# Queries and keys of a head pair kept in three orders, copied on GpSimd, so that attention scores are read with unit step

## The chip, the core and the metric

The kernel runs on one core of a Trainium2 chip. A core has five engines that work side by side, each through its own queue in order: TensorE (PE, matrix products; its weight loads are shown apart as PEld), VectorE (DVE), ScalarE (ACT), GpSimd (POOL), and SyncE (SP), which here mostly issues transfers (DMA) between HBM and the on-chip memory SBUF. Products land in PSUM, a small accumulator memory. The metric is the device time of one execution in microseconds (us).

## The reference

One encoder layer over a prompt of 256 and a sample of 2048 tokens with the same weights. After an input projection, half of the columns go through a Hyena mixer (two long convolutions, done here by Fourier transforms as matrix products), the other half through dilated attention. The attention is what the change touches:

```python
DILATED_BRANCHES = ((128, 1), (512, 4), (2048, 16))
def by_residue(a):
    return a.reshape(B, Ls, dilation, H, E).transpose(0, 2, 1, 3, 4)
...
s = jnp.einsum('brnqhe,brnkhe->brnhqk', qb, kb).astype(jnp.float32) * (E ** -0.5)
...
s = jnp.where(valid[None, None, :, None], s + bias[None, None, None], NEG_INF)
m = jnp.max(s, axis=-1, keepdims=True)
p = jnp.exp(s - m)
```

There are 8 heads of 64 channels. In a branch with dilation d, token t attends to tokens with the same residue t mod d, within a window. So the branches read queries and keys with step 1, 4 and 16. The three outputs are merged by their softmax denominators, joined with the Hyena half, normed, projected and fed to a gated feed-forward.

## The kernel before

Code is written as generators that `weave` emits side by side; a scheduler then fixes the order of each engine's queue. After the input projection the attention (`attention`) and the Hyena convolutions (`hyena`) are woven; the output projection (`output`) and the feed-forward follow. The output works in nine blocks of 256 tokens: the first is the prompt, and the other eight need the finished Hyena result of the sample.

**Attention.** Heads are taken in four pairs (`hp`), each pair in three branches (`b`). A pair and a branch make a section of 18 blocks of 128 queries. Of these, 16 belong to the sample and two to the prompt; in the first branch all read with step 1, in the second the sample's read with step 4 and in the third with step 16. The prompt's two blocks in the second branch are "packed" ones read with step 2, and so are those of the third.

`prepare` loads queries and keys of a head, channel by token, into three tiles of 128 partitions and 2304 columns: `Qh` (rounded queries), `Ql` (the rest) and `Ks` (keys, rounded on half of the partitions, the rest on the other half). It works in four chunks of 576 columns: transfers on SP, a rounding on ACT (L861, L864), differences on DVE (L201, tile Ql) and POOL (L201, tile Ks), a cast on DVE (L866). The next pair is prepared during the current one, a step every sixth block. The tiles of one pair lie in one place, those of the next in another, so that two sets exist.

`scores` makes a block: per head two matmuls into tile aS (L901 with Qh as weights and Ks moving, L902 with Ql), then a sum with the bias and its minimum on DVE (L905, to tile aP), and the exponential with its sum on ACT (L908). aS has two buffers. `flip` transposes aP on PE (L917, tile aT) and copies it out on ACT or DVE; `values` multiplies by the values (L932, tile aOp); `tokens` transposes back (L945, aOT) and stores.

**Hyena.** For each convolution, `hyena_first` is the first transform step: DVE casts and a POOL difference (L201, tile hS), matmuls L689 and L690, a copy, a store. `hyena_second` goes through groups: 32 for the sample, 4 for the prompt. A group has the product hs2k (L720, the filter's spectrum), a scaling on DVE (L722, tile hK), the product hs2z (L724, the signal's), four DVE products (L728 to L731, into tiles t1 and t2, both shown as ht), their addition on POOL (L732), and the first inverse step hs3 on PE (L738) with a copy on ACT. hs2k and hs2z share two PSUM buffers, and t2 has one. Then a last step per row of the inverse: L775 on PE (hs4), L776 on DVE. The second convolution starts when the first one's result has gone through all its first steps. Two groups share one load each of the transform's table (htab), the signal (hx) and the filter (hk) and one store of hbe; hx, hk, hbe and the last step's hD are tiles of 128 partitions by 2 by 512 in float32. A last step also loads the gate and stores the result, each half as large as hD.

Of the kernel before, what the change touches and what calls it, by code (L numbers as in the profile page):

```python
# [21 lines left out]
P = 128  # L22
# [10 lines left out]
# ---------------------------------------------------------------- constants of the shapes  # L33
# [106 lines left out]
# ---------------------------------------------------------------- host layout  # L140
# [46 lines left out]
# ---------------------------------------------------------------- the kernel  # L187
class Hybrid:
# [20 lines left out]
    # ---- constants that live through the whole kernel  # L209
# [33 lines left out]
    # ---- emission of several parts of the kernel side by side  # L243
    def weave(self, streams, until=None):
        """streams: [[generator, yields expected, yields so far]]; ends with `until`, or with all of them."""
# [12 lines left out]
    # ---- modulation: columns of silu(c) @ ada_w + ada_b for one of the six parts  # L258
# [10 lines left out]
    def ada_tensor(self, pool, psp):  # L269
        """Part 1 and the first half of part 0 on the tensor engine."""  # L270
# [25 lines left out]
    def ada_vector(self, s, pool, rows, bufs, ms=range(8)):  # L296
        """Part s on the vector engine, from the transposed weights."""
# [10 lines left out]
    # ---- Hyena filters: position MLP, decay, norm, spectrum  # L308
# [157 lines left out]
    # ---- input projection  # L466
    # a sub-block: (first column of xT, number of columns)
# [30 lines left out]
    def input_rstd(self, wp, w2, psp, p):  # L498
        """1 / rms over the channels of x, on every partition, for the columns that pass p is the first to use."""
# [19 lines left out]
    def first_input(self, wp, w2, psp):  # L519
        """Normed x of the first pass, with its 1 / rms."""  # L520
# [18 lines left out]
    def modulate(self, X, both=False):  # L539
        """x * (gain * (1 + scale)) + shift."""  # L540
# [21 lines left out]
    def split(self, hp, X, H):  # L562
        """hi + lo = x."""
# [20 lines left out]
    def project(self, hp, wp, w2, psp, ms, H=None):  # L584
        """Columns `ms` (in chunks of 128) of the input projection, for all tokens; H: input of the first pass."""
# [77 lines left out]
    # ---- Hyena: long convolutions of one request and one order  # L663
    def time_major(self, t, r, q):
        """Rows token = n2c * i + nh * h + q, q + 1 of a token-major DRAM tensor, by h as [i, 2, c]."""
        off, L = REQ[r]
        nh = L // 128
        v = t[off:off + L].rearrange("(i h n) c -> h i n c", h=2, n=nh)
        return [v[h, :, q:q + 2] for h in range(2)]
# [6 lines left out]
    def hyena_first(self, wp, psp, r, An, n, z):  # L676
        """First DFT step, over the rows of z, for the columns n and n + 1 of each half."""
# [17 lines left out]
    def hyena_second(self, wp, psp, r, o, A, B):  # L695
        """Second DFT step of the signal and of the filter, their product, first inverse step."""
# [988 lines left out]
```

## Time and profile before

| what | value |
|---|---|
| time, three runs | 3507.36, 3507.86 (median), 3508.28 us |
| span of the profiled execution | 3512.3 us |
| PE busy | 3281.4 us, 93% |
| DVE busy | 2633.7 us, 75% |
| ACT busy | 1548.2 us, 44% |
| POOL busy | 1430.0 us, 41% |
| attention with Hyena beside it | 945 to 1646 us of the span |

The profile lists no time of the profiled execution other than its span, which is 0.13% over the median. A busy PE is not PE at its peak: matmuls are pipelined, so the duration of one overlaps the next, and a matmul's price is read from its start to the start of what follows. Shares over the whole span mix stages with different limits; the stretch from 945 to 1646 us is the one to look at.

### The profile page before, as it was taken

What the parts mean: (1) busy time and instruction counts of PE and PEld (TensorE: products, weight loads), DVE (VectorE), ACT (ScalarE), POOL (GpSimd) and SP (SyncE); (2) the same over time, 40 slices, a digit from 0 to 9 for tenths busy, and PEclk for the clock granted to TensorE, in tenths of its full rate; (3) what the DMA queues carried; (4) which work ended last, traced back from release to release, by engine and by line L of the source; (5) the groups of instructions that cost most, each with busy time, mean ns of one, the idle gap of its engine ahead of it and who ended that gap; (6) DMA issues with size and microseconds to landing.
All of it is one profiled execution on the core that took longest, in us unless ns stands there. A gap on an engine that the chain in (4) does not pass through costs nothing.

```text
span 3512.3 us, 57891 instructions
## 1 busy us (share of the span) xinstructions
PE 3281.4 (93%) x21142; PEld 2941.1 (84%) x21142; DVE 2633.7 (75%) x4490; ACT 1548.2 (44%) x3190; POOL 1430.0 (41%) x1110
## 2 busy tenths in 40 slices
PE   7999899899899899998899899999899999899998
PEld 4987788789756666565799799999899999899998
DVE  7988878765487667685887878888887878567657
ACT  4576743323254665455554433223332324344433
POOL 1487761124231332220444555545655555223222
PEclk9999999999999999999899899999999999999999
DMA  6454557676675766658576523445433224456655
GB/s 243 133 173 131 149 179 233 220 234 198 189 212 171 212 198 201 195 176 258 182 218 183 202 94 112 148 152 181 184 140 141 96 96 157 167 194 228 210 186 175
DMA packets 407828, 628.08 MB, mean 179 GB/s; under 512 B 27919, under 2 KB 230927, under 8 KB 401623
## 3 DMA queue, kind: packets, MB, share of 16 engines
q1 hardware_dynamic: 354384, 593.13, 51.5%
q10 hardware_dynamic: 52072, 28.40, 2.7%
q8 instruction: 168, 2.75, 0.3%
q0 software_dynamic: 1088, 2.85, 0.2%
q14 instruction: 116, 0.95, 0.1%
HBM read 419.03 MB, written 205.25 MB: 178 GB/s over the span
## 4 chain that ended last, share of the span: by engine, by line
PE 34%; DVE 8%; DMA 3%; issue 3%; POOL 3%; ACT 1%; ACTq 0%; SPq 0%; DVEq 0%; POOLq 0%
PE w L207 6%; PE w L206 6%; PE w L205 6%; PE fd L207 5%; PE fd L206 4%; PE fd L205 4%; DMA wraw<-in_w_gate 1%; POOL gs L1422 1%; DVE wlo L201 1%; DVE hl L201 1%; DMA hl<-d_opT 1%; DVE fT L1259 1%; DVE cv L1455 1%; DVE cv L1444 1%; DMA d_x1T<-ox 0%
## 5 line engine op out<-in xcount | busy, mean ns | idle before, releaser
L207 PE MATMUL w<-hh,wlo 128*128 128x290 f32 (+1 forms) x2464 | 733.4, 300 | 21.3 <-DVE wlo L201 17.2
L205 PE MATMUL w<-hh,whi 128*128 128x288 f32 (+1 forms) x2464 | 731.9, 298 | 12.9 <-ACT whi L1353 10.4
L206 PE MATMUL w<-hl,whi 128*128 128x288 f32 (+1 forms) x2464 | 736.8, 300 | 4.4 <-DVE hl L201 4.4
L207 PEld LDWEIGHTS w<-hh,wlo 128*128 128x128 f32 x2464 | 470.6, 192 | 26.2 <-DVE wlo L201 20.8
L205 PEld LDWEIGHTS w<-hh,whi 128*128 128x128 f32 x2464 | 471.0, 191 | 14.3 <-ACT whi L1353 11.1
L206 PEld LDWEIGHTS w<-hl,whi 128*128 128x128 f32 x2464 | 472.1, 192 | 4.9 <-DVE hl L201 4.9
L205 PE MATMUL pj<-hThi,wihi 128*128 128x386 f32 (+1 forms) x1152 | 403.2, 350 | 6.1 <-ACT u L626 4.1
L206 PE MATMUL pj<-hTlo,wihi 128*128 128x386 f32 (+1 forms) x1152 | 401.3, 349 | 7.9 <-DVE hTlo L201 7.9
L207 PE MATMUL pj<-hThi,wilo 128*128 128x386 f32 (+1 forms) x1152 | 398.5, 346 | 0.0
L207 PE MATMUL fd<-hh,dwl 128*128 128x288 f32 x1210 | 359.8, 297 | 5.7 <-DVE dwl L201 5.7
L205 PE MATMUL fd<-hh,dwh 128*128 128x288 f32 x1210 | 360.2, 298 | 1.8 <-ACT dwh L1550 1.8
L206 PE MATMUL fd<-hl,dwh 128*128 128x288 f32 x1210 | 357.9, 296 | 0.0
L732 POOL TENSOR_TENSOR ht<-ht,ht 128x512 f32<-128x512 f32 x72 | 94.4, 1311 | 453.4 <-DVE ht L731 374.5
L1353 ACT CAST whi<-ws 128x512 fp32r<-128x512 f32 x176 | 109.3, 621 | 318.6 <-PE w L206 294.9
L206 PEld LDWEIGHTS pj<-hTlo,wihi 128*128 128x128 f32 x1152 | 222.3, 193 | 20.5 <-DVE hTlo L201 9.8
L205 PEld LDWEIGHTS pj<-hThi,wihi 128*128 128x128 f32 x1152 | 221.5, 192 | 17.1 <-ACT u L626 4.4
L207 PEld LDWEIGHTS fd<-hh,dwl 128*128 128x128 f32 x1210 | 228.3, 189 | 6.0 <-DVE dwl L201 5.9
L207 PEld LDWEIGHTS pj<-hThi,wilo 128*128 128x128 f32 x1152 | 221.4, 192 | 13.2 <-issue 8.8
L205 PEld LDWEIGHTS fd<-hh,dwh 128*128 128x128 f32 x1210 | 230.2, 190 | 2.4 <-ACT dwh L1550 2.0
L206 PEld LDWEIGHTS fd<-hl,dwh 128*128 128x128 f32 x1210 | 229.7, 190 | 0.4
L908 ACT ACTIVATE aP<-aP,aO 128x256 f32<-128x256 f32 (+2 forms) x432 | 194.1, 451 | 57.4 <-DVE aO L905 47.2
L201 POOL TENSOR_TENSOR hl<-hl,hh 128x576 fp32r<-128x576 f32 (+1 forms) x66 | 113.2, 1723 | 247.8 <-ACT hh L1492 184.1
(302 smaller groups left out, 8287.2 us busy)
## 6 DMA issues: line engine op xcount, KB each, us to landing
hl<-d_G SPq DMA_DIRECT2D x154, 288.0 KB, 5.4
dwl<-d_S SPq DMA_DIRECT2D x59, 704.0 KB, 4.1
wiraw<-in_w_in SPq DMA_DIRECT2D x72, 512.0 KB, 4.4
d_G<-cv SPq DMA_DIRECT2D x42, 576.0 KB, 2.8
wraw<-in_w_gate SPq DMA_DIRECT2D x22, 1024.0 KB, 5.1
wraw<-in_w_up SPq DMA_DIRECT2D x22, 1024.0 KB, 4.9
adat<-in_ada_t SPq DMA_DIRECT2D x36, 512.0 KB, 4.3
d_fA<-fae SPq DMA_DIRECT2D x72, 256.0 KB, 2.8
```

The source lines that it names most:

```text
L201: eng.tensor_tensor(out=lo, in0=x, in1=hi.bitcast(F32), op=ALU.subtract)
L205: mm(out, wh, xh, start=first, stop=False)
L206: mm(out, wh, xl, start=False, stop=False)
L207: mm(out, wl, xh, start=False, stop=last)
L732: nc.gpsimd.tensor_tensor(out=t1, in0=t1, in1=t2, op=ALU.add)
L908: nc.scalar.activation(sb[:, hh, :n], sb[:, hh, :n], AF.Exp, scale=-1.0, bias=mn, accum_out=dn)
L1259: v.tensor_tensor(out=o, in0=x, in1=y, op=ALU.subtract)
L1353: nc.scalar.copy(hi, x)
L1422: nc.gpsimd.tensor_tensor(out=G[k][:, h, s1 - o:e1 - o], in0=u[:, s1 - s:e1 - s], in1=cv[k].rearrange("p (t e) -> p e t", e=2)[:, h, s1 - ...
L1444: nc.vector.scalar_tensor_tensor(out=cv[k][:, s2:e], in0=gs[k][:, own + s2 - 1:own + e - 1], scalar=w[:, 0:1], in1=cv[k][:, s2:e], op0=ALU ...
L1455: nc.vector.tensor_tensor(out=o, in0=x, in1=y, op=ALU.subtract)
```

## The change

Instead of reading the natural order with a step, each section gets its own tiles in its own order: natural for the first branch, by residue mod 4 for the second, by residue mod 16 for the third. A new generator `by_residue` makes them on POOL: the second branch's from the natural tiles (reads with step 4), the third's from the second's (again reads with step 4). It is 15 copies per head and section (three tiles, four residues of 512 columns, and the prompt's 256 columns as they are), 30 for a pair, for 8 of the 12 sections. Tiles now alternate between the two places from section to section instead of from pair to pair, and the natural tiles of the next pair are loaded within the third branch's section. `scores` then reads consecutive columns; the packed blocks stay as they were.

```diff
+    def by_residue(self, src, dst, b):
+        cp = self.nc.gpsimd.tensor_copy
+        for res in range(4):
+            part = slice(LP + 512 * res, LP + 512 * res + 512)
+            for x, y in zip(src, dst):
+                if b == 1:
+                    i, o = x[:, LP + res::4], y[:, part]
+                else:
+                    i = x[:, part].rearrange("p (j a) -> p a j", a=4)
+                    o = y[:, LP:].rearrange("p (a r j) -> p r a j", a=4, r=4)[:, res]
+                cp(o, i.bitcast(F32))
+            yield
+        for x, y in zip(src, dst):
+            cp(y[:, :LP], x[:, :LP].bitcast(F32))
...
-                t0 = off + res + dil * P * j
-                qs = slice(t0, t0 + dil * (P - 1) + 1, dil)
                 if kind == "win":
+                    at = off + res * (L // dil)
+                    qs = slice(at + P * j, at + P * j + P)
...
-                    m0 = off + res + dil * k0
-                    rhs = Ks[:, m0:m0 + dil * (n - 1) + 1:dil]
+                    rhs = Ks[:, at + k0:at + k0 + n]
                 elif kind == "res":
+                    qs = slice(off + P * res, off + P * res + P)
...
-                    e = res - res % 2
-                    rhs = Ks[:, off:off + L].rearrange("p (j s) -> p s j", s=dil)[:, e:e + 2]
+                    e = off + P * (res - res % 2)
+                    rhs = Ks[:, e:e + 2 * P]
...
+            if u % 3:
+                gens = [self.by_residue(src[hh], out[hh], u % 3) for hh in range(2)]
+            else:
+                gens = [self.prepare(2 * (u // 3) + hh, out[hh]) if u or hh else self.pre for hh in range(2)]
...
+                u = 3 * hp + b
+                if u == 11:
+                    mq.close()
+                heads, nxt = nxt, []
+                ahead = iter(()) if u == 11 else prepare(u + 1, heads, nxt) if u else chain(own, prepare(1, heads, nxt))
```

What the scheduler makes of it is shown at two places. The first is POOL's queue in the first section. Names carry the buffer's number; Ks differences (L201) belong to the loading of a pair, L732 is a Hyena group's addition. Before:

```order
L201 TENSOR_TENSOR Ks_9470<-Ks_9470,kh_9513 64x576
L732 TENSOR_TENSOR ht1_6724<-ht1_6724,ht2_6725 128x512
L201 TENSOR_TENSOR Ks_9470<-Ks_9470,kh_9562 64x576
L732 TENSOR_TENSOR ht1_6741<-ht1_6741,ht2_6742 128x512
L201 TENSOR_TENSOR Ks_9470<-Ks_9470,kh_9629 64x576
L732 TENSOR_TENSOR ht1_6841<-ht1_6841,ht2_6842 128x512
```

And after, with L880 the copies of 512 columns and L883 those of 256; seven further copies like the first stand where the dots are:

```order
L201 TENSOR_TENSOR Ks_9470<-Ks_9470,kh_9513 64x576
L880 CAST Ql_9688<-Ql_8902 128x512
L880 CAST Ks_9689<-Ks_8903 128x512
L880 CAST Qh_9690<-Qh_8904 128x512
...
L880 CAST Ks_9689<-Ks_8903 128x512
L880 CAST Qh_9690<-Qh_8904 128x512
L883 CAST Ql_9688<-Ql_8902 128x256
L732 TENSOR_TENSOR ht1_6724<-ht1_6724,ht2_6725 128x512
L201 TENSOR_TENSOR Ks_9470<-Ks_9470,kh_9562 64x576
```

The addition of group 6724 moved from right behind the difference of the keys to behind thirteen copies.

The second place is PE's queue at the end of the first output block (om is the output projection, ot its transposes, rstd a norm's sum). Before:

```order
L206 MATMUL om_15773<-oml_15587,ow_15496 128x256
L207 MATMUL om_15773<-omh_15586,ow_15496 128x256
L1182 MATMUL ot_15717<-ident_60,ohy_15653 128x128 x4
L1182 MATMUL ot_15724<-ident_60,oat_15667 128x128 x4
L1182 MATMUL ot_15731<-ident_60,ohy_15682 128x128 x4
```

And after:

```order
L206 MATMUL om_16235<-oml_15875,owh7_15930 128x256
L207 MATMUL om_16235<-omh_15874,owl7_15931 128x256
L689 MATMUL hs1_9302<-hS_9296,hf11_5117 128x512
L690 MATMUL hs1_9302<-hS_9296,hf11_5117 128x512
L1293 MATMUL rstd_16493<-oacc_16059,ones_65 128x256
L689 MATMUL hs1_9306<-hS_9296,hf11_5117 128x512
L690 MATMUL hs1_9306<-hS_9296,hf11_5117 128x512
L724 MATMUL hs2z_9323<-hx_9315,htab_9313 128x512
L720 MATMUL hs2k_9403<-hk_9317,htab_9313 128x512
L724 MATMUL hs2z_9407<-hx_9315,htab_9313 128x512
L738 MATMUL hs3_9416<-ht1_9325,htab_9313 128x512
```

From there the order after goes on with the products of 32 Hyena groups and 16 last steps (L775), and only then with the transposes of the second output block; before, these stand between the attention's blocks.

## Rows read from the trace of the kernel before

**Rows 1.** Busy time by stretch: us, PE, PEld, DVE, ACT, POOL, clock, DMA, GB/s.

```profile
945.00:1646.00 701.00, 660.19 (x3732) 434.19 (x3732) 496.83 (x1475) 383.97 (x1235) 173.79 (x124) 0.97 0.67 202
...
946.00:1020.00 74.00, 62.78 (x318) 36.15 (x317) 61.48 (x141) 43.82 (x111) 27.59 (x19) 0.88 0.85 232
...
1253.00:1295.00 42.00, 41.63 (x244) 30.22 (x243) 23.13 (x104) 23.58 (x94) 12.14 (x9) 1.00 0.64 190
1295.00:1343.00 48.00, 40.40 (x321) 28.72 (x318) 39.11 (x117) 38.26 (x108) 22.08 (x15) 1.00 1.01 282
```

**Rows 2.** PE's timeline: start us, us, line, operation, out<-in, shapes, count, idle before.

```profile
961.30 0.39 PE L901 MATMUL aS<-Ks,Qh 128*128 128x256 f32 x1
...
961.88 0.38 PE L917 MATMUL aT<-ident,aP 128*128 128x128 f32 x2
...
1071.40 0.60 PE L901 MATMUL aS<-Ks,Qh 128*128 128x256 f32 x1
...
1072.53 0.62 PE L917 MATMUL aT<-ident,aP 128*128 128x128 f32 x4
...
1118.71 1.02 PE L738 MATMUL hs<-ht,htab 128*128 128x512 f32 x2
1119.57 1.02 PE L720 MATMUL hs2k<-hk,htab 128*128 128x512 f32 x2
```

**Rows 3.** POOL's operations by line, whole trace: duration ns min/median/max.

```profile
L421 POOL MEMSET acc<- x4: 525/545/566, 133.4 to 321.8; 128x512 f32 x4
...
L732 POOL TENSOR_TENSOR ht<-ht,ht x72: 1261/1275/2062, 578.0 to 1574.1; 128x512 f32<-128x512 f32 x72
...
L201 POOL TENSOR_TENSOR ow<-oraw,ow x3: 2381/2382/2401, 1478.6 to 1500.6; 128x1024 fp32r<-128x1024 f32 x3
```

**Rows 4.** Groups by line and shape, 945 to 1646: busy us, mean ns | idle before.

```profile
L722 DVE TENSOR_TENSOR hK<-hs2k,hrn 128x512 f32<-128x512 f32 x59 | 40.7, 689 | 8.8 <-PE hs2k L720 6.4 <-DMA hrn<-d_rnc 1.3
L905 DVE CUSTOM_DVE_ANT_0 aP<-aS,aB 128x128 f32<-128x128 f32 x160 | 39.6, 286 | 37.9 <-PE aT L917 31.1 <-issue 3.9 <-PE aS L902 2.6
L905 DVE DVE_READ_ACCUMULATOR2_ANT aO<- 128x1 f32 x432 | 35.2, 81 | 0.0
L201 DVE TENSOR_TENSOR Ql<-Ql,Qh 128x576 fp32r<-128x576 f32 x27 | 23.7, 878 | 1.3 <-ACT Qh L861 1.2
L866 DVE CAST Ks<-Ks 64x576 fp32r<-64x576 f32 x27 | 22.2, 823 | 11.8 <-DMA Ks<-d_kT 11.8
...
L908 ACT ACTIVATE aP<-aP,aO 128x256 f32<-128x256 f32 x176 | 88.2, 503 | 20.1 <-DVE aO L905 18.3 <-DMA hk<-d_fA 1.0 <-ACT aPT L921 0.2
L908 ACT ACTIVATION_READ_ACCUMULATOR aP<-aP,aO 128x1 f32 x432 | 81.7, 189 | 0.0
```

**Rows 5.** Timelines of PE and POOL where Hyena steps and output follow each other.

```profile
905.12 0.40 PE L690 MATMUL hs<-hS,hf 128*128 128x512 f32 x1
...
919.06 1.29 POOL L732 TENSOR_TENSOR ht<-ht,ht 128x512 f32<-128x512 f32 x1 [23.28 <-DVE ht L731]
...
1574.11 1.28 POOL L732 TENSOR_TENSOR ht<-ht,ht 128x512 f32<-128x512 f32 x1 [4.94 <-DVE ht L731]
...
1588.63 1.08 PE L775 MATMUL hs<-hD,hgi 128*64 128x512 f32 x4
...
1643.45 0.66 PE L945 MATMUL aOT<-ident,aOC 128*128 128x128 f32 x4
...
1660.69 1.08 PE L775 MATMUL hs<-hD,hgi 128*64 128x512 f32 x4
...
1684.61 0.56 PE L205 MATMUL om<-omh,ow 128*128 128x256 f32 x1
```

**Rows 6.** Transfers issued from 945 to 1646: count, KB each, median us to landing.

```profile
hD<-d_hB SPq DMA_DIRECT2D x32, 512.0 KB, 5.3
...
hk<-d_fA SPq DMA_DIRECT2D x29, 512.0 KB, 4.6
...
htab<-in_tab SPq DMA_DIRECT2D x29, 256.0 KB, 3.9
```

More of the change, by code (lines that the diff above doesn't have):

```diff
@@ L2 @@
 from contextlib import ExitStack
-from itertools import islice
+from itertools import chain, islice
 import numpy as np
@@ L965, in store, with tiles, prepare @@
             return go
-        def prepare(hp, out):
+        def tiles(u, hh):
+            return self.qk_tiles(wp, 6) if u % 2 else self.qk_tiles(self.ow if hh else self.qkp, 3)
+        def prepare(u, src, out):
             for hh in range(2):
-                if hp or hh:
-                    out.append(self.qk_tiles(wp, 6) if hp % 2 else self.qk_tiles(self.ow if hh else self.qkp, 3))
-            gens = [self.prepare(2 * hp + hh, out[hh]) if hp or hh else self.pre for hh in range(2)]
-            for _ in range(4):
+                if u or hh:
+                    out.append(tiles(u, hh))
+            if u % 3:
+                gens = [self.by_residue(src[hh], out[hh], u % 3) for hh in range(2)]
+            else:
+                gens = [self.prepare(2 * (u // 3) + hh, out[hh]) if u or hh else self.pre for hh in range(2)]
+            for _ in range(5):
                 for x in gens:
@@ L979, in attention @@
         nxt = [first]
-        own = prepare(0, nxt)
+        own = prepare(0, None, nxt)
         next(own)
@@ L983, in attention @@
         for hp in range(4):
-            if hp == 3:
-                mq.close()
             cs = slice(hp * P, hp * P + P)
-            heads, nxt = nxt, []
-            ahead = prepare(hp + 1, nxt) if hp < 3 else iter(())
-            yield
             for b in range(3):
-                dil = DILS[b]
+                u = 3 * hp + b
[3 more added lines that the diff above has]
+                ahead = iter(()) if u == 11 else prepare(u + 1, heads, nxt) if u else chain(own, prepare(1, heads, nxt))
+                yield
                 lo = (0, 256, 640)[b]
@@ L1002, in attention @@
                         res, j, nb = blk
-                        if hp == 0:
-                            next(own, None)
+                        if u == 0 and k < 8:
+                            next(ahead, None)
                         sb, n = scores(heads, g, i, blk, ot, bias, b)
@@ L1008, in attention @@
                         if kind == "win":
-                            x["v"], x["vs"] = vbase[r] + j * dil + res, dil
+                            x["v"], x["vs"] = vbase[r] + j * DILS[b] + res, DILS[b]
                         else:
@@ L1012, in attention @@
                         k += 1
-                        if k % 6 == 0:
+                        if u or k > 6:
                             next(ahead, None)
@@ L1025, in attention @@
                             values(q2.pop(0))
-            for _ in ahead:
-                pass
+                for _ in ahead:
+                    pass
         for y in q1:
```

## The prediction

> **What bounds the kernel now.** I read the busy times by stretch first, then TensorE's timeline inside one stretch, then the groups by line and the transfers. The change touches the attention, from 945 to 1646 us. There PE is busy 660 of 701 us, DVE 497, ACT 384, POOL 174 [rows 1]; in 1253 to 1295 PE has 41.6 of 42 us [rows 1]. So PE sets the pace, and POOL is the idle engine. Attention is twelve sections of 18 blocks (four head pairs, three branches); the Hyena convolutions run between the blocks.
>
> One block's scores are four matmuls. Read with unit step (first branch) they take from 961.30 to 961.88, the start of the next work: 0.58 us. Read with step 4 they take from 1071.40 to 1072.53: 1.13 us [rows 2]. Twice as long, and PE is the bound: a real price.
>
> **What the change takes away.** 16 of 18 blocks in two of three branches of four pairs become unit step: 128 blocks. The packed blocks keep step 2. 128 x (1.13 - 0.58) = 70 us of PE. That is the whole gain, and it counts only where PE stays the bound.
>
> **What it adds: copies on POOL.** Each of 8 sections copies three tiles of two heads: 24 copies of 512 columns and 6 of 256, 192 and 48 in all. No row shows a copy on POOL, nor a read with step 4. Bounds for 512 columns: a fill takes 0.545 us [rows 3]; a two-input operation of 1024 columns, as if each strided element cost two, takes 2.38 us [rows 3]. The two-input one of 512 takes 1.275 us [rows 3]. [...] A section then has 24 x 1.3 + 6 x 0.7 = 35.4 us of copies, plus two Hyena additions of 1.275 us: 38 us of POOL. One section's copies write tiles that the section before last still reads, so they start when that one's scores end and must end when the next begins: 38 us is as long as a section of PE work (below). The cover is thin: at 1.6 us a copy, POOL is the bound by 6 us in each.
>
> [...]
>
> **What it moves: the Hyena.** This decides my forecast. The scheduler's order shows that in the section with copies only one or two Hyena groups are left, because each group's addition stands on POOL behind a dozen copies; see the order of POOL. When the last attention block is issued, the order before has all 72 groups of the second DFT step behind it; the order after has 40, and the other 32 stand on PE behind the first output block, with no attention work between them, followed by 16 last steps. Before, this work hid between attention blocks. Now it is a tail. Output blocks two to nine need all of it.
>
> **The attention, after.** PE: 660 us busy, minus 70, minus 32 groups x 3 matmuls x 0.86 us (1118.71 to 1119.57 [rows 2]) = 83, minus some 29 for steps moved behind (13 last steps of the second convolution, and 8 steps with a last and a first step's matmuls, about 1.0 us each kind): 478 us, 40 a section. In a copying section ACT has 36 exponentials of up to 0.503 us with 0.189 us of read-out each [rows 4], 25 us, and 9 of copies: 34. With PE 40, POOL 38 and ACT 34, all in order, I take 42. In the sections that load the next pair, two have seven groups on DVE: a group is one product of 0.689 us and four alike, on half the partitions [rows 4], 3.43 us, so 24 us; 36 score operations of 0.286 + 0.081 = 13; eight splits of 0.878 and eight casts of 0.823 = 14 [rows 4]; about 6 of copies: 57 us, more than PE's. I take 56. The first section (74 us now, DMA share 0.85 [rows 1]) loses four of nine groups: 62. The third loading section, with two groups, 45; the last 32. Sum: 62 + 7 x 42 + 2 x 56 + 45 + 32 = 545 us.
>
> **The tail, after.** First output block with the rest of the first steps: as now from 1643.45 to 1684.61 [rows 5], 42 us. From the last first step to the first group's addition: 905.12 to 919.06 [rows 5], less one group: 11. Groups alone: DVE 3.43 us, plus what it waits for hs2z, whose buffer its own last product frees: 0.86 + 0.2 - 0.69 = 0.4. Two groups move a table of 256 KB and, by their equal tiles, three pieces as large as hk's 512 KB [rows 6], 1792 KB; at the 282 GB/s of a stretch with DMA share 1.01 [rows 1] that is 6.5 us, 3.3 a group, so DVE rules and landings add a little: 4.1. 32 x 4.1 = 131. Last group to first last step: 1574.11 to 1588.63 [rows 5], 14. 16 last steps: 512 KB of hD [rows 6], half as much for the gate and half for the result, 1 MB: 3.7 us at the same rate, more than PE's 1.08 [rows 5] and DVE's 0.69 together. I take 3.8: 61. Last step to the second output block: 1660.69 to 1684.61 [rows 5], less a step: 23. Sum: 282 us.
>
> **The sum.** 545 + 282 = 827 us. The same way now, from 946 to 1685, is 739 us. So +88 us. The profiled execution's span, 3512.3 us, is 4.4 us over the median 3507.9; the difference is put on the median: 3595 us, rounded. The output and the feed-forward behind it keep their work.
>
> **The rivals.** (1) Even: a copy costs under 1 us and hides, and PE's sum decides the attention except in the first section, 490 us; the groups in the tail take 3.5 us. Tail 42 + 9 + 112 + 12 + 57 + 20 = 252. Together 742, +3: 3511 us. For it: PE lost 0.4 us of 42 in 1253 to 1295 [rows 1], with all other engines at half load; against it: here ACT, POOL or DVE would stand close to PE. (2) Faster: each engine works off its lag in the next section, so that attention costs PE's sum alone, 478, and the tail DVE's and the transfers' sums without hand-overs: 35 + 9 + 110 + 11 + 55 + 20 = 240. That is 718 us, -21: 3487 us. Its place is DVE's queue in the two crowded sections and in the tail; it decides where all losses over these sums stay under 21 us. Against it: scores have two buffers, so DVE can't lag by more than two blocks, and the groups wait for their own buffer. (3) POOL is the bound: at 2.0 us a copy (and 1.0 for the small) a section has 48 + 6 + 2.5 = 57 us, 58 with the hand-over. Seven sections cost 16 us more each: attention 657, tail as above, +200: 3708 us. For it: nothing in the trace excludes it, and each Hyena addition ties DVE and PE to POOL's queue. (4) That the change does not do what it says: the packed blocks aside, the order shows the score matmuls on the copied tiles; I give it nothing of its own.
>
> **How the numbers follow.** Forecast, with attention 515 to 590 and tail 258 to 310: 0.70, from +34 to +161, 3542 to 3669, likeliest 3595 us. Even 0.08, faster 0.11, POOL-bound 0.11. A measurement of this kernel can tell about 0.2%, 7 us, from no change. The even case lies around its +3 and gives 0.02 to faster, 0.05 to same and 0.01 to slower; the forecast's lower edge gives 0.02 to same: faster 0.13, same 0.07, slower 0.80. The range from 3500 to 3670 leaves out most of the faster case (0.09), most of the POOL-bound one (0.08) and reaches over the forecast's own.
>
> **What would show it.** Right: four score matmuls of a step-4 block in 0.58 us from start to next work; last attention matmul at about 1490 us instead of 1643; behind the first output block some 130 us in which PE is busy about two thirds, with the Hyena products on DVE and no score work; second output block at about 1770. A copy of 512 columns near 1.3 us, and POOL busy about 90% in copying sections. Wrong: copies of 0.6 us with sections still at 42 (then ACT or the in-order coupling is the cause); copies of 2 us (rival 3); groups at 3.5 us in the tail, or attention's end before 1440 us (rivals 1 and 2); score matmuls as slow as before (then the step was not their price).

## The result, and the profile after

The changed kernel takes 3686.5 us (median of four, 3681.1 to 3687.5), the kernel before 3507.6 us: ratio 1.0505, 95% interval 1.0493 to 1.0518. It is slower by 179 us. The prediction said 3595 us, slower by 88, in a range that ended at 3670. The direction and its reason hold; the size doesn't.

First TensorE's timeline of the kernel after: a block whose scores were read with step 4 before, the last score, and the start of the second output block (start us, length us, engine, line, operation, tiles, shapes, count):

```profile
1104.85 0.36 PE L917 MATMUL aS<-Ks,Qh 128*128 128x256 f32 x1
1105.05 0.28 PE L918 MATMUL aS<-Ks,Ql 128*128 128x256 f32 x1
1105.17 0.28 PE L917 MATMUL aS<-Ks,Qh 128*128 128x256 f32 x1
1105.29 0.28 PE L918 MATMUL aS<-Ks,Ql 128*128 128x256 f32 x1
1105.41 0.38 PE L933 MATMUL aT<-ident,aP 128*128 128x128 f32 x2
...
1532.44 0.28 PE L918 MATMUL aS<-Ks,Ql 128*128 128x256 f32 x1
...
1874.25 1.01 PE L205 MATMUL om<-omh,ow 128*128 128x256 f32 x3
```

The same two places, the last score and the second output block, in the kernel before:

```profile
1638.37 0.40 PE L902 MATMUL aS<-Ks,Ql 128*128 128x256 f32 x1
...
1705.03 0.28 PE L206 MATMUL om<-oml,ow 128*128 128x256 f32 x1
```

Four score matmuls go from 1104.85 to 1105.41, 0.56 us instead of 1.13 [rows 2]: the change does what it says. The attention ends 106 us earlier than before, and yet the second output block starts at 1874, which in the kernel before it did at 1705.0 (seven of its 192 matmuls stand among those of the first block there, from 1692.2 on). That is the loss: +169 us at this point, +173 at the end of the profiled executions (3685.7 to 3512.3).

Busy time by stretch of the kernel after (stretch, length, PE, PEld, DVE, ACT, POOL, granted clock, DMA share, GB/s): the attention, from there to the first leftover Hyena group, the 32 groups, the 16 last steps, and the rest.

```profile
946.00:1532.00 586.00, 494.22 (x3399) 333.23 (x3398) 374.23 (x1265) 355.43 (x1183) 339.58 (x320) 0.92 0.53 155
1532.00:1624.00 92.00, 59.94 (x308) 41.91 (x306) 51.50 (x96) 24.13 (x50) 35.12 (x27) 0.76 0.65 194
1624.00:1791.00 167.00, 106.88 (x184) 34.35 (x184) 107.06 (x156) 18.17 (x31) 39.26 (x31) 0.91 0.50 163
1791.00:1874.00 83.00, 36.27 (x81) 8.13 (x82) 15.54 (x22) 5.95 (x14) 3.00 (x2) 0.51 0.72 228
1874.00:3685.00 1811.00, 1729.88 (x12786) 1713.44 (x12785) 1390.49 (x2039) 683.63 (x1162) 825.73 (x696) 0.98 0.48 163
```

From 1532 to 1874 no engine is near its limit: PE 59%, DVE 51% over the 342 us, DMA share between 0.50 and 0.72. Where no engine and no transfer is near its limit and nothing else covers the waits, the time is likely to go to hand-overs from one engine to the next. In the 32 groups this chain can be read operation by operation:

```profile
1661.93 1.27 POOL L732 TENSOR_TENSOR ht<-ht,ht 128x512 f32<-128x512 f32 x1 [2.81 <-DVE ht L731]
...
1663.26 1.77 PE L738 MATMUL hs<-ht,htab 128*128 128x512 f32 x2 [0.78 <-DVE hK L722]
...
1664.82 1.91 PE L724 MATMUL hs2z<-hx,htab 128*128 128x512 f32 x2
...
1668.87 0.69 DVE L731 TENSOR_TENSOR ht<-hs2z,hK 64x512 f32<-64x512 f32 x1
...
1669.71 1.27 POOL L732 TENSOR_TENSOR ht<-ht,ht 128x512 f32<-128x512 f32 x1 [6.51 <-DVE ht L731]
1669.71 1.35 PE L724 MATMUL hs2z<-hx,htab 128*128 128x512 f32 x2 [1.92 <-DVE ht L731]
1671.03 2.08 PE L738 MATMUL hs<-ht,htab 128*128 128x512 f32 x2
...
1674.04 1.27 POOL L732 TENSOR_TENSOR ht<-ht,ht 128x512 f32<-128x512 f32 x1 [3.06 <-DVE ht L731]
```

At 1663.26 PE does hs3 (line 738) of the group whose addition POOL has just finished, and only then hs2z (line 724) of the next group, for which DVE waits. So DVE, POOL and PE work one after the other, and the next addition comes 7.8 us later (the granted clock was 0.74 from 1661 to 1674; most intervals of this kind take 6.3). At 1669.71 hs2z stands ahead of hs3, runs beside the addition, and the next one comes after 4.3 us. Over the tail most intervals are 4.1 and 6.3 us in turn; 31 of them take 166.75 us, 5.38 a group.

### The profile page after: what moved, and what is told of

Read it like the earlier page. It is cut to its first block, busy times and chain, and to the rows that moved or that the text cites. A ratio compares the mean times of both kernels' runs of the same rounds, so it can differ in the third digit from the quotient of the medians.

```text
span 3685.7 us, 58220 instructions
## 1 busy us (share of the span) xinstructions
PE 3282.5 (89%) x21142; PEld 2892.5 (78%) x21142; DVE 2654.2 (72%) x4490; ACT 1549.3 (42%) x3194; POOL 1647.5 (45%) x1350
## 4 chain that ended last, share of the span: by engine, by line
PE 59%; DVE 17%; DMA 11%; issue 5%; POOL 4%; ACT 3%; SPq 2%; DVEq 0%; POOLq 0%; ACTq 0%
PE w L207 7%; PE w L206 7%; PE w L205 7%; PE fd L207 4%; PE fd L206 4%; PE fd L205 4%; PE pj L206 2%; PE pj L205 2%; PE pj L207 2%; PE aOp L948 2%; DMA adat<-in_ada_t 2%; PE aT L933 2%; PE hs2z L724 2%; PE aS L917 2%; PE hs L738 1%
## 5 line engine op out<-in xcount | busy, mean ns | idle before, releaser
L732 POOL TENSOR_TENSOR ht<-ht,ht 128x512 f32<-128x512 f32 x72 | 96.0, 1334 | 427.2 <-DVE ht L731 375.2
L201 POOL TENSOR_TENSOR hl<-hl,hh 128x576 fp32r<-128x576 f32 (+1 forms) x66 | 112.7, 1715 | 244.9 <-ACT hh L1515 201.1
```

The costliest lines, as they stand in the source:

```text
L201: eng.tensor_tensor(out=lo, in0=x, in1=hi.bitcast(F32), op=ALU.subtract)
L732: nc.gpsimd.tensor_tensor(out=t1, in0=t1, in1=t2, op=ALU.add)
```

## The experiments

Medians in us of each run and of the kernel before, timed beside it on the same chip, with their ratio:

| run | us | before | ratio, 95% interval |
|---|---|---|---|
| unit_only | 3453.5 | 3505.5 | 0.985 (0.983 to 0.986) |
| unit_k | 3498.6 | 3509.2 | 0.997 (0.996 to 0.998) |
| unit_spare | 3507.4 | 3507.8 | 0.999 (0.998 to 1.000) |
| unit_jit | 3467.7 | 3505.2 | 0.990 (0.988 to 0.991) |
| unit_spare_dve | 3504.6 | 3505.2 | 1.000 (0.999 to 1.001) |
| copies_old_steps | 3691.8 | 3505.5 | 1.053 (1.052 to 1.055) |
| lag2 | 3586.0 | 3505.5 | 1.023 (1.022 to 1.025) |
| before_lag2 | 3488.2 | 3507.8 | 0.994 (0.992 to 0.996) |
| pieces4 | 3629.4 | 3507.8 | 1.034 (1.032 to 1.037) |
| add_dve | 3609.9 | 3511.3 | 1.029 (1.026 to 1.031) |
| copy_act | 3610.1 | 3505.5 | 1.029 (1.028 to 1.031) |
| copy_dve | 3562.8 | 3509.2 | 1.016 (1.014 to 1.017) |
| q_av | 3529.1 | 3507.8 | 1.006 (1.004 to 1.008) |
| q_av_lag | 3516.7 | 3505.2 | 1.004 (1.002 to 1.005) |
| before_nosim | 3833.0 | 3509.2 | 1.093 (1.091 to 1.095) |
| after_nosim | 3875.7 | 3509.2 | 1.104 (1.103 to 1.106) |
| before_nosim_add | 3819.6 | 3511.3 | 1.088 (1.087 to 1.090) |
| after_nosim_add | 3885.9 | 3511.3 | 1.108 (1.105 to 1.110) |

**The gain alone** (unit_only), and the keys' part of it (unit_k, which keeps the old `qs`). Edit to the kernel before:

```diff
-                t0 = off + res + dil * P * j
-                qs = slice(t0, t0 + dil * (P - 1) + 1, dil)
...
+                    at = off + res * (L // dil)
+                    qs = slice(at + P * j, at + P * j + P)
...
-                    m0 = off + res + dil * k0
-                    rhs = Ks[:, m0:m0 + dil * (n - 1) + 1:dil]
+                    rhs = Ks[:, at + k0:at + k0 + n]
```

> The kernel before, its order included, with the scores of the second and third branch read with unit step from the tiles in natural order and no copies (so they multiply other columns than the reference's). It measures the gain alone. Theory 1 (TensorE sets the pace of the attention, and the step doubles the score matmuls): 128 blocks x 0.55 us = 70 us less, about 3438 us, up to 3455 if DVE comes out as the bound where nine Hyena groups fall into one section. Theory 2 (the gain was never there, because other engines stand close behind TensorE): 3490 to 3508 us.

> The kernel before, its order included, without copies; keys (the moving side of the score matmul) are read with unit step, queries (its weights) with the old steps (other columns than the reference's). It tells which side's step has the price. Weights alone: no gain, 3505 us, the matmuls still 0.24 us from start to start. Moving side alone: 3453 us, as with both in unit step. I expect the weights: start to start was 0.24 us for 192 and 256 columns alike.

Measured: 52 us less than before for both sides, at the upper end of theory 1; 11 us for the keys alone (7 to 16 by the interval). The gain is real. The groups of score matmuls and weight loads by line (out<-in, shapes, count | busy us, mean ns), first both in unit step, then keys alone:

```profile
L901 PE MATMUL aS<-Ks,Qh 128*128 128x256 f32 (+1 forms) x432 | 149.4, 367 | 8.1 <-DVE aO L905 8.0
...
L902 PEld LDWEIGHTS aS<-Ks,Ql 128*128 128x128 f32 x432 | 83.9, 194 | 11.1 <-issue 10.7
```

```profile
L903 PE MATMUL aS<-Ks,Qh 128*128 128x256 f32 (+1 forms) x432 | 179.7, 424 | 6.4 <-DVE aO L907 6.2
...
L904 PEld LDWEIGHTS aS<-Ks,Ql 128*128 128x128 f32 x432 | 116.5, 270 | 8.3 <-issue 4.9 <-DMA Ks<-d_kT 0.2
```

A weight load takes 194 ns from queries in unit step (they are the weights of the score matmul) and 270 as a mean with the old steps. The 41 us between the two runs are not the queries' alone, though. In the second branch the score matmuls of 256 columns follow each other (median) after 0.24 us in the kernel before and in unit_k, and after 0.23 in q_av below, where the queries are in unit step and the keys are not; only with both in unit step it is 0.12. A step on either side alone keeps most of TensorE's price.

**Copies on POOL that nobody reads** (unit_spare, added to unit_only). Edit:

```diff
+        def spare(heads, b):
...
+                        y = wp.tile([P, 256], mybir.dt.bfloat16, tag="sp", name="sp", bufs=1)
+                        nc.gpsimd.tensor_copy(y, x[:, part].bitcast(F32))
...
+                        next(idle, None)
```

> The kernel before with unit step on the natural tiles (other columns than the reference's), plus copies on POOL that nobody reads: in seven of the eight copying sections 48 of 256 columns, read with step 4 from the section's tiles into a scratch tile of half the width. So POOL has the copies' load, but no score waits for a copy and the next pair is loaded as early as before. No Hyena group is left behind the attention. Theory 1 (POOL's time costs nothing by itself): 3453 plus 0 to 20, about 3465 us. Theory 2 (a busy POOL slows DVE or the others): 3520 us or more.

Measured: 54 us over unit_only, between the two forecasts. Where it went decides. TensorE's timeline of unit_only, last score and last Hyena step, and then of unit_spare, with the start of its second output block:

```profile
1580.06 0.28 PE L902 MATMUL aS<-Ks,Ql 128*128 128x256 f32 x1
...
1603.01 1.17 PE L775 MATMUL hs<-hD,hgi 128*64 128x512 f32 x4
```

```profile
1581.67 0.28 PE L902 MATMUL aS<-Ks,Ql 128*128 128x256 f32 x1
...
1669.93 1.97 PE L775 MATMUL hs<-hD,hgi 128*64 128x512 f32 x4 [5.41 <-DVE hg L776]
...
1688.09 1.01 PE L205 MATMUL om<-omh,ow 128*128 128x256 f32 x3
```

The attention ends at the same time, within 2 us, with POOL busy 400 us between 945 us and that point instead of 172. The Hyena chain ends 67 us later: all sixteen last steps stand behind the last score instead of five, and the output waits for them. So POOL's load did not lengthen the attention; it cost by holding Hyena up. At the second output block 41 of the 53 us between the two profiled executions are there (1688.1 against 1646.8); the other 12 come behind it and are not explained. Theory 2's mechanism, a DVE slowed by POOL, is a small part: three groups on DVE that move in SBUF alone (L866, the differences into Ql, the casts into hS) took 8 us more in total, of which none shows in the attention's end. Of all runs this is the cleanest, since loads and scores are untouched.

**Does the attention's length matter after the change?** copies_old_steps is the changed kernel with before's `t0`, `m0` and steps put back on the copied tiles.

> The changed kernel with all its copies, but the scores read the copied tiles with the old steps of 4 and 16 (other columns than the reference's). Its order leaves the same 32 Hyena groups behind the attention as the changed kernel's. Against the changed kernel it puts back what the unit step saves. Theory 1 (TensorE sets the pace of the sections that copy; those that load wait for other engines): 35 us in the second branches and about 15 of 35 in the third, so about 3735 us (3715 to 3756). Theory 2 (POOL's copies set the pace): 3686 to 3700 us.

Measured: 3691.8, 5 us over the changed kernel, against the 49 that theory 1 expected. The last score comes at 1559.6 instead of 1532.4, the second output block at 1877.2 instead of 1874.3. So 27 us of longer attention are 3 us at the second output block: what stands in between was hardly waiting for the attention. The number is theory 2's, its mechanism is not: the old steps did lengthen the attention. What sets the end is neither the score matmuls nor the copies' own time in the sections, but the Hyena chain beside them.

**The chain itself.** lag2 issues the last matmul of a group two groups later; before_lag2 does the same to the kernel before.

```diff
-        for g in range(n2c + 1):
+        for g in range(n2c + 2):
...
-            if prev is not None:
-                g2, tb, pp = prev
+            if prev2 is not None:
+                g2, tb, pp = prev2
...
+            prev2 = prev
             prev = cur
```

> The changed kernel with the last matmul of a Hyena group (hs3) issued two groups later instead of one; all else as changed, 32 groups still behind the attention. In the changed kernel's tail every second group has hs3 ahead of the next group's hs2z on TensorE, so that hs2z waits for POOL's addition of the group just made (intervals of 6.3 and 4.3 us in turn). Theory 1 (that order is what makes a group cost 5.38 instead of 4.1 us): about 4.1 us a group, 40 us less, 3647 us. Theory 2 (the transfers of a pair, into one buffer for hk, set 10.7 us a pair): 3686 us, the same intervals.

> The kernel before with the last matmul of a Hyena group two groups later, as in lag2. It has no groups alone behind the attention. If the 100 us of lag2 came from Hyena's chain being late and slow in the changed kernel, nothing changes here: 3500 to 3510 us. If the later matmul helps the attention in general, 3480 us or less.

Measured: lag2 is 100 us faster than the changed kernel, where 40 were expected; before_lag2 is 20 us faster than before, between its two forecasts. TensorE and POOL of lag2 in its tail:

```profile
1638.92 1.27 POOL L733 TENSOR_TENSOR ht<-ht,ht 128x512 f32<-128x512 f32 x1 [2.81 <-PE hs2k L721]
...
1642.95 1.27 POOL L733 TENSOR_TENSOR ht<-ht,ht 128x512 f32<-128x512 f32 x1 [2.77 <-DVE ht L732]
1642.96 1.10 PE L725 MATMUL hs2z<-hx,htab 128*128 128x512 f32 x2 [1.26 <-DVE ht L732]
...
1644.28 1.12 PE L739 MATMUL hs<-ht,htab 128*128 128x512 f32 x2 [0.22 <-POOL ht L733]
...
1646.98 1.10 PE L725 MATMUL hs2z<-hx,htab 128*128 128x512 f32 x2 [0.66 <-PE hs2k L721]
1647.03 1.27 POOL L733 TENSOR_TENSOR ht<-ht,ht 128x512 f32<-128x512 f32 x1 [2.81 <-DVE ht L732]
```

hs2z now always stands ahead, and additions follow each other after 4.03 and 4.08 us; from the ninth interval on all are 4.0 or 4.1 (in the first eight, 4.1 to 6.4, TensorE also works on the first output block and is busy 90%). So it was not the transfers that set the pace, as theory 2 had it, but the order of two matmuls. In the tail that gives 29 us (137.6 us for 31 intervals instead of 166.75). The larger part is that the tail starts 66 us earlier (first addition 1558.1 instead of 1624.3): 7 us of it before the attention, 24 in an attention that is itself shorter, and 36 between its end and the first addition. The same chain runs through the whole attention, and there too it was late. In before_lag2 the attention is as long as before, and the last Hyena step comes at 1623 instead of 1661. **before_lag2, at 3488 us, is faster than both kernels.**

**Getting Hyena forward in other ways.** pieces4 cuts each copy on POOL into four; add_dve puts Hyena's addition (line 732) on DVE.

```diff
-                cp(o, i.bitcast(F32))
+                for h in range(4):
...
+                        cp(o[:, w * h:w * h + w], i[:, w * h:w * h + w].bitcast(F32))
```

```diff
-                nc.gpsimd.tensor_tensor(out=t1, in0=t1, in1=t2, op=ALU.add)
+                nc.vector.tensor_tensor(out=t1, in0=t1, in1=t2, op=ALU.add)
```

> The changed kernel, all copies on POOL, each of 512 columns cut into four of 128: the same columns moved, but an addition of Hyena's can stand between two short copies. In its order 5 Hyena groups are left behind the attention instead of 32. Theory 1 (the loss is mostly Hyena's additions kept behind POOL's long copies): what remains is what the copies on DVE also cost outside the copying sections (loads just in time in three sections, about 48 us, and a longer last section, 10) on the 3453 us of unit step alone, plus 5 groups: 3520 to 3550 us. Theory 2 (copies and loads cost in the sections themselves, whatever Hyena does): 3640 us or more.

> The changed kernel, with the plan on, and Hyena's additions on DVE. In its order 17 groups are left behind the attention instead of 32. Theory 1 (Hyena's additions behind POOL's copies): 15 groups of 5.4 us less and no POOL in a group's chain, 80 to 110 us less than the changed kernel, 3575 to 3605 us. Theory 2: 3660 us or more, the additions only loading DVE.

Measured: 57 and 77 us less than the changed kernel, both short of theory 1's range (by 79 and by 5 us). Fewer groups left behind means less time in both, but not in proportion: behind the last score come 6 additions in pieces4 and 18 in add_dve, instead of 32. pieces4 shows a second cost. Its copies are dear (0.42 us for 128 columns, four of them 1.68 instead of 1.13), and its three loading sections take 90, 82 and 90 us.

**Copies on other engines.** copy_act and copy_dve change only `cp`; with both, every Hyena group is back inside the attention.

> The changed kernel with all copies on ACT instead of POOL; its order has every Hyena group inside the attention again, as before. Theory 1 (the loss is the Hyena work that the copies on POOL pushed behind the attention): the gain of the unit step comes through, less what ACT's queue costs now (192 copies of some 0.59 and 48 of some 0.4 us, the length of an ACT copy of 128x512, added to an ACT that was busy 384 of 701 us): about 3455 us (3437 to 3490). Theory 2 (copies cost what they cost wherever they stand, by the new chain from copy to scores): 3530 us or more.

> The changed kernel with all copies on DVE; its order has all Hyena groups inside the attention, as before. On ACT a copy that reads with step 4 took 1.11 us, as on POOL (1.13). Theory 1 (a copying engine hurts as far as its queue fills beside the work it has): if DVE takes 0.55 us a copy, 24 of them add 13 us to the 23 to 50 that DVE has in a copying section, within 10 us of TensorE's: 3453 plus 10 to 25, about 3470 us. If DVE takes 1.1 us as well, 27 us on 50 beside TensorE's 60 in five sections of eight: 3453 + 5 x 17 = 3538 us. Theory 2 (the chain from copy to scores costs by itself): 3600 us, like the copies on ACT.

Measured: 3610 and 3563 us. Both are slower than before, by 2.9 and 1.6%, so displaced Hyena work is not the only price; copy_act has theory 2's number. Copies of 512 columns by engine (operation, tiles, count, duration ns min/median/max, first and last start), on POOL in the changed kernel, on ACT and on DVE:

```profile
L880 POOL CAST Ks<-Ks x64: 1075/1127/1647, 949.9 to 1463.1; 128x512 fp32r<-128x512 f32 x64
```

```profile
L880 ACT CAST Ks<-Ks x64: 1082/1107/1177, 948.6 to 1651.2; 128x512 fp32r<-128x512 f32 x64
```

```profile
L880 DVE CAST Ks<-Ks x64: 590/618/1853, 955.1 to 1595.7; 128x512 fp32r<-128x512 f32 x64
```

On ACT the copy is nearly twice the 0.59 us I took from an ACT copy of the same shape, and with the small copies (0.41 us) 29 us a section stand in the queue of the exponentials. On DVE it is 0.62 us, near the cheap one of my two prices, some 16 us a section; yet the run came out above the figures for both (3470 and 3538).

**What is left of copy_dve's 110 us over unit_only.** unit_jit has loads as late as the change needs them and no copies; unit_spare_dve has unread copies on DVE and early loads.

```diff
-                        if k % 6 == 0:
+                        if b == 2:
+                            if g is groups[0] and i == 0 and hp < 3:
...
+                                        nc.vector.tensor_copy(t[:, 0:NT:576], sb[:, 0, 0:4])
```

> The kernel before with unit step on the natural tiles (other columns than the reference's), no copies, but the next pair's queries and keys loaded only in the third section of the pair, as the change has to: six small DVE writes of four columns each tie the loads to that section's first block. Theory 1 (loads just in time are the larger part of what the copies on DVE cost over unit step alone, where the three loading sections were 48 us longer): 3453 + 50 = 3503 us (3490 to 3515). Theory 2 (the loads hide as well there): 3470 us or less, and the copies themselves make the 110.

> The kernel before with unit step on the natural tiles (other columns than the reference's), with unread copies as in unit_spare, but on DVE: 48 of 256 columns in seven sections, some 15 us of DVE in each at 0.31 us. Loads as early as before, Hyena as before. Theory 1 (most of the copies' cost on DVE was loads just in time): 3453 plus 30 to 45, about 3490 us. Theory 2 (DVE's time is the cost): 3453 plus 7 x 13 = 3545 us.

Measured: the late loads cost 14 us, the unread copies on DVE 51 (0.39 us for 256 columns, 336 of them, 131 us of DVE). My theory that the loads were the larger part falls (unit_jit has theory 2's number; unit_spare_dve lies between the two forecasts); the copies' own time in DVE's queue is. 44 us belong to neither alone and stay open; scores that wait for copies, and copies and loads in one section, are possible and were not run apart.

**With the scheduler's plan off** (`schedule_with_timeline_sim=False` in both kernels), where no Hyena work is left behind in either, and again with the additions on DVE:

> The kernel before, with the scheduler's plan by simulated times turned off, so that instructions stand by their place in the program text and its weave. It is the partner of the next run. 40 of the 72 Hyena groups stand ahead of the attention, the rest are spread over its first eight sections. No forecast of the absolute time rests on rows; 3500 to 3650 us.

> The changed kernel with the same plan turned off: all copies stay on POOL, but the Hyena groups stand where they stand in the partner (40 ahead of the attention, the rest in its first eight sections, none behind it). Theory 1 (the copies cost what they cost because Hyena's additions and subtractions queue behind them and the second convolution comes out behind the attention): here the gain of the unit step is left, 20 to 52 us less than the partner. Theory 2 (copies on POOL cost in the attention sections themselves, wherever Hyena stands): 20 us or more above the partner.

> The kernel before with the plan by simulated times off, and Hyena's additions on DVE instead of POOL. Partner of the next run; POOL's additions cost TensorE no wait in before_nosim, so about 3833 us, 3825 to 3850.

> The changed kernel with the plan off and Hyena's additions on DVE, so that none of them stands behind a copy on POOL. Theory 1 (the additions behind POOL's copies are the cause: with the additions on POOL, TensorE waited 31.9 us for them, against nothing in the partner): the 43 us over the partner go down to +10 or below, to -20 if the clock comes back with the waits. Theory 2 (the copies and the late loads cost in the sections by themselves): still +30 us or more over the partner.

Measured: without the plan the kernel before takes 3833 us, 183 over the range expected, and 3820, 5 under its range, with the additions on DVE. The change costs 43 us with the additions on POOL and 66 with them on DVE. Theory 1's numbers fail in both, and theory 2's (20 and 30 us or more) are met. But the traces show that the pair did not separate the two. TensorE's waits in after_nosim from 1358 to 1866 (who waits for what: us in total, times, longest); the partner has no such wait among its seven largest:

```profile
PE hs L738 <- POOL ht L732: 31.9, 7, 11.5
```

And in after_nosim_add DVE's timeline, then POOL's over the same time:

```profile
1310.52 0.36 DVE L921 CUSTOM_DVE_ANT_0 aP<-aS,aB 128x192 f32<-128x192 f32 x1
1310.81 0.08 DVE L921 DVE_READ_ACCUMULATOR2_ANT aO<- 128x1 f32 x1
1310.81 21.11 DVE L732 TENSOR_TENSOR ht<-ht,ht 128x512 f32<-128x512 f32 x1
1331.84 0.35 DVE L921 CUSTOM_DVE_ANT_0 aP<-aS,aB 128x192 f32<-128x192 f32 x1
```

```profile
1310.66 1.18 POOL L880 CAST Ql<-Ql 128x512 fp32r<-128x512 f32 x1
1311.70 1.18 POOL L880 CAST Ks<-Ks 128x512 fp32r<-128x512 f32 x1
...
1328.19 1.12 POOL L880 CAST Qh<-Qh 128x512 fp32r<-128x512 f32 x1
1329.22 0.43 POOL L883 CAST Ql<-Ql 128x256 fp32r<-128x256 f32 x1
...
1330.94 0.43 POOL L883 CAST Qh<-Qh 128x256 fp32r<-128x256 f32 x1
```

The addition that takes 0.68 us otherwise took 21.11, until POOL's row of copies was through, and DVE's score work waited behind it. So these traces put the additions behind POOL's copies either way: in POOL's queue (31.9 us of TensorE's waits), or on DVE beside them (21.11 us). What I meant as a kernel free of that cause was not, and the runs can't be read as proof of theory 2, nor of theory 1. How much of the 43 us is the late loads and the copies themselves stays open.

**Queries only** (q_av, q_av_lag): keys stay natural, queries are copied in turn on ACT and DVE.

```diff
-            for x, y in zip(src, dst):
+            for x, y in zip(src[::2], dst[::2]):
...
-                cp(o, i.bitcast(F32))
+                cps['av'[k % 2]](o, i.bitcast(F32))
+                k += 1
...
-                    rhs = Ks[:, at + k0:at + k0 + n]
+                    m0 = off + res + dil * k0
+                    rhs = Ks[:, m0:m0 + dil * (n - 1) + 1:dil]
```

> A version that might beat both: only the queries (the weights of the score matmuls) are put in residue order, the keys stay natural and are read with step, since the step of the keys cost 7 us of 52; the keys of the next pair are loaded a section earlier than its queries; copies in turn on ACT and DVE (8 each of 512 columns a section), none on POOL. Hyena's groups are all inside the attention. Unit step of the queries alone leaves about 3461 us; ACT gets 9 and DVE 5 us a section more, and half the loads stay just in time: 50 to 60 us of the 110 that the copies on DVE cost. 3495 to 3545 us, about 3515: even with before.

> The queries-only version with copies on ACT and DVE, with the last Hyena matmul two groups later, which took 19 us off the kernel before: 3529 - 19 = 3510 us (3495 to 3515). It beats the kernel before with that alone, 3488 us, only if copies of the queries cost less than the 45 us that they bring.

Measured: 21 and 11 us slower than before, the first in its range, the second 2 us over it. It loses least of all versions whose copies are read. But it does not have the gain that it was built for. The scores of a block of the second branch in q_av, and its weight loads:

```profile
1039.57 0.47 PE L933 MATMUL aS<-Ks,Qh 128*128 128x256 f32 x1
...
1040.56 0.62 PE L949 MATMUL aT<-ident,aP 128*128 128x128 f32 x4
```

```profile
L934 PEld LDWEIGHTS aS<-Ks,Ql 128*128 128x128 f32 x432 | 89.6, 207 | 13.9 <-issue 11.4 <-DMA Ks<-d_kT 0.3
```

The four matmuls take 0.99 us, against 1.13 before and 0.56 in the changed kernel, although the weights are loaded in 207 ns. All score matmuls together keep TensorE busy 340 us, against 353 before, 332 in unit_k and 268 in unit_only. So the expectations' 45 us for the queries alone are not there: as long as the keys are read with a step, most of TensorE's price stays, and the copies come on top.

## Why the prediction was right and wrong

**Right.** That PE saves about 70 us: 68 in unit_only (from 945 us to the last score PE is busy 654 us before, 586 there), of which 52 reach the end. The copy: 1.13 us, forecast 1.3, so rival 3 (POOL is the bound) is out; so is rival 4. No run shows the 1.3 and 0.7 us a copy behind the forecast's 35.4 us of copies a section; the runs showed 1.13 and 0.41 us, which make 29.6. The seven copying sections: 293 us, forecast 7 x 42 = 294. There is luck in that sum: single sections take 37 to 48 us, PE is busy 84 to 97% of them and POOL 58 to 84, where about 90 was expected. That 32 groups and 16 last steps would run alone, and that this would make the change slower. The last steps: 54.7 us between the first and the last of the rows there, forecast 61 for all.

**The base.** "The same way now, from 946 to 1685" is the first failed step. The row at 1684.61 [rows 5] is not the second output block but a later part of the first; the second starts at 1705.0. The order shown as the end of the first output block before has the same slip: its transposes stand behind the first 48 of that block's 192 matmuls. The same way was 759 us and not 739, so the forecast's own 827 us were worth +68, not +88: about 3575 us. It was wrong by more than it looks.

**The terms that were too small.** Against the 928.3 us from 946 to 1874 the sum of 827 is short by 101. Sections are taken from first score to first score. First section 55.1 (forecast 62); loading sections 60.0 + 73.1 + 59.8 = 192.9 (forecast 157, +36); last section 45.6 (forecast 32, +14); from the last score to the first addition 91.9 (forecast 42 + 11 = 53, +39); groups 166.75 (forecast 131, +36); the rest of the tail 83 (forecast 98, -15).

The groups: "DVE rules and landings add a little: 4.1" is the step that failed. 4.0 to 4.1 is what lag2 showed once hs2z stood ahead of hs3; the sum had DVE's work and the transfers, but not the order of the two matmuls on PE, which puts POOL's 1.27 us and hs3 into DVE's path in every second group. It took 5.38 us a group.

The stretch of 92 us between: "First output block with the rest of the first steps: as now" took it that the first steps are nearly done when the attention ends. They weren't. After the change the last steps of the first convolution run from 1380 to about 1600, in the kernel before from 1172 to 1330. This is the structural fault. I added an attention and a tail, one behind the other. In the changed kernel the end is set by one Hyena chain that runs beside the attention all the way, and the attention only has to be over by then. copies_old_steps (27 us more attention, 3 us at the second block) and unit_spare (same attention, Hyena 67 us later) show it from two sides; lag2 (the tail 66 us earlier, with an attention 24 us shorter) agrees. So a section's length was the wrong thing to work out; the question was how far the Hyena chain gets in a section. For the same reason the differences above are those of a sum, and not causes that add up.

The loading sections are explained in part: late loads alone made 14 us (unit_jit), seven groups stand in the longest, and the granted clock in the three was 0.89, 0.81 and 0.86; what makes up the rest was not settled.

**The account.** From unit_only to the changed kernel are 233 us. Some 30 us of unread POOL work a section cost 54; late loads 14; the rest is put down to the full displacement and its interplay with loads and copies, which no run takes apart. That POOL's copies slowed DVE is a rival that the changed kernel's trace bounds: from 940 us to the second output block the casts into hS (L684) took 21.3 us instead of 14.3, and no other group of the attention or the Hyena on DVE grew by more than 1.1 us in total. Single changes that move Hyena forward take back 57, 77 and 100 us; they overlap and don't add up.

**Rivals 1 and 2** needed the copies hidden and all lags absorbed: an attention of 490 or 478 us and groups of about 3.5. Measured were 586 and 5.38; the lags of Hyena had no slack behind them to be absorbed in.

## What to carry to other kernels

Before pricing what an edit adds to an idle engine, ask whose small operations already stand in that engine's queue, and follow their chain to the end: POOL was a quarter busy, but every Hyena group passed through it, and that chain set the end of the changed kernel. A second stream that fills gaps is itself a critical path once its cover gets shorter, so make it robust first: one more group between addition and matmul was worth 100 us in the changed kernel, 20 in the kernel before, and some 10 in the queries-only version. And measure the gain without its cost (unit step on the natural tiles, no copies) before building the cost: 52 us was all that the unit step brought here. And measure it for each half before building half of it: keys alone brought 11 us, and queries alone left most of the score matmuls nearly as slow as they were.

## What the runs showed of the hardware

- A DVE addition of two SBUF tiles stretched from 0.68 to 21.11 us beside a row of copies on POOL; eight of 72 took over 1.4 us in after_nosim_add, together 73 us too long, and four in add_dve (the longest 15.05). In before_nosim_add, where POOL makes no copies, the longest takes 1.83 us. DVE's score operation, which reads PSUM and SBUF, showed no stretch: the 176 of 256 columns took 73.8 us in the changed kernel, none over 0.43, and 73.2 in the kernel before. The 21.11 us lasted over some twenty copies in a row; what holds the addition beside them is not shown.
- A copy of 512 columns that reads with step 4 took 1.13 us on POOL, 1.11 on ACT and 0.62 on DVE; 256 in unit step took 0.41 on POOL.
- A step in either operand of a score matmul kept most of its price on TensorE: in the second branch the matmuls of 256 columns followed each other (median, granted clock 1.00) after 0.24 us with a step on both sides (the kernel before), 0.24 with a step in the weights alone (unit_k), 0.23 with a step in the moving side alone (q_av), and 0.12 with none (unit_only). For 192 columns it was 0.24, 0.24, 0.18 and 0.11: from 192 to 256 columns it grew most with the step in the moving side alone. The weight loads there took 0.31, 0.31, 0.21 and 0.19 us.
- In the 83 us of last steps at the end of the tail the granted clock was 0.51; in the groups before them it was 0.91, with PE busy 64%, and PE then waited 7.8 us for the first step's data. What lowered the clock is not shown. A group of four matmuls on line 775 took 1.97 us there, 1.08 in the kernel before [rows 5]. The steps came every 3.65 us, so PE's matmuls alone did not set their pace.
